# Folding kept partial sums by accumulating transfers instead of VectorE adds, and draining two kept sums earlier

## The chip, the core and the metric

The kernel runs on one core of a Trainium2 chip. The metric is the device time of one execution in microseconds (us); lower is better. The core has a matrix engine (TensorE, "PE" in the profile, with its weight loads "PEld"), a vector engine (VectorE, "DVE"), a scalar engine (ScalarE, "ACT"), a general engine (GpSimd, "POOL") and a sync engine ("SP") which here only issues transfers. All of them run their own instruction list in order and meet at semaphores. Matrix products are written to PSUM, eight banks of 128 x 512 floats; everything else lies in SBUF or in the chip's main memory.

## What is computed

Two decoder layers over 256 tokens of width 2048, in float32. Layer 0 has a short gated convolution, layer 1 latent attention; both end in the same kind of MLP with a squared ReLU, and each sub-layer in a layer norm:

```python
def sq_relu_mlp(x, w1, w2):
    return jnp.square(jax.nn.relu(x @ w1)) @ w2
...
        h = layer_norm(ALPHA * h + mix, ln_g[layer, 0], ln_b[layer, 0])
        h = layer_norm(ALPHA * h + sq_relu_mlp(h, mlp_w1[layer], mlp_w2[layer]),
                       ln_g[layer, 1], ln_b[layer, 1])
```

`w1` is 2048 x 8192 and `w2` is 8192 x 2048. The change touches the MLP of both layers only.

## The kernel before

**Precision.** Every weight that comes in as float32 (`raw`) is split into a rounded part (`hi`, a cast on ACT, L139) and the rest (`lo`, a subtraction on DVE, L140). A product is made of three matmuls: hi by hi, lo by hi, hi by lo. So each 512 KB of weights costs ACT one cast and DVE one 128 x 1024 subtraction.

**The MLP.** The 8192 hidden columns are walked in eight quarters of 1024, numbered q = 0 to 7, each in eight units m = 0 to 7 of 128 columns. A slot (q, m) makes one unit of the first product (`ps_u`, L256 and L260), which ACT and DVE take out of PSUM into `fp` (L401, L402), and, five units behind, one pair of the second product. For the quarters 1 to 6 (`FAST`, in layer 1 also for half of quarter 7) the second product is done by a seven-product scheme in the manner of Strassen: the weights of a pair are combined on DVE (L172, L177, L179), and seven products named "1" to "7" each gather in their own PSUM bank. The output columns are in two groups, g = 0 and g = 1.

**Changes of groups.** At slot (q, 0), q = 2 to 7, the seven banks pass from one group to the other. What they hold is put back into SBUF and what the other group had is brought in. Products "1", "5", "7" and "6" are kept in the tile `sums`, the others in `acc`. ACT copies five of them out (L659) and in (L747). "6" and "4" (`ADDED`) start from zero after a change, and DVE adds them to what is kept: `sums += ps` and `acc += ps`, both at L657. The function `move` takes one entry of the list `moves` at a time, at fixed places of a slot: four at the end of the slot that closes a group, the rest after each single weight of the next slot and behind `evacuate`. Since the list goes by the order 3, 1, 5, 7, 2, 6, 4, the two adds of DVE come last.

**Folds.** When quarter 6 has closed a group, the kept sums are combined by eight dependent adds of 128 x 512 (`fold`, L667): s6 += s1, s7 += s6, then six adds onto blocks of `acc`. `fold` is a generator and `fold_some(n)` runs n of its steps. In layer 0, the eight adds of group 0 run at slot (7, 4) and those of group 1 at (7, 6) and (7, 7). In layer 1 only group 0 is folded so, three adds at (7, 7), two in the slot behind it, and the rest at the end; group 1 is folded with the last products (`fold_last`, L678).

**What hangs on the folds.** In layer 0 the tile `sums` lies in the space of the residual (`xres`). The residual was stored to main memory (`parked`, L895) and comes back as `xback` (L914) by four transfers that POOL issues; they can start only when no fold reads `sums` any more. DVE scales the first part of `xback` (L454), and a matmul on it (`mu0p`, L456) stands in PE's list between the products of the last quarter (`ps_d`). In layer 1 ACT copies the folded blocks of `acc` into PSUM (`last_sum`, `ps_e<-acc`, L685), and the products of the last quarter gather on top.

**Order.** Within the slots the list of each of PE, DVE and ACT is fixed as written (`Order.keep`); POOL and SP, and everything behind the slots, are placed by a scheduler when the program is built. All weights come through seven buffers of 512 KB, loaded by SP.

Of the kernel before, what the change touches and what calls it, by code (L numbers as in the profile page):

```python
# [13 lines left out]
ALU = mybir.AluOpType  # L14
# [8 lines left out]
NQ = 8  # L23
QC = FF // NQ // P
# [13 lines left out]
SHIFT = 5  # L38
# [18 lines left out]
def trunk(ctx: ExitStack, tc: tile.TileContext, xT, vecs, lead, w_first, w_in, w_out, w_kv, w_q, w_uk, w_uv,  # L57
          w_qn, w_qp, w_o, w1, w2, w2f, cosT, sinT, mask, ident, gb, out):
    nc = tc.nc
# [53 lines left out]
    class Banks:  # L113
# [15 lines left out]
        @classmethod  # L129
        def next(cls):  # L130
            cls.count += 1
            return (cls.count - 1) % (4 if cls.more is None else 8)
# [59 lines left out]
    def size(i):  # L192

        return 1 if len(stream[i]) == 1 else 6
# [187 lines left out]
    OWN = ("1", "5", "7", "6")  # L382
# [8 lines left out]
    def fast_products(ps, x, j, fresh, ready, onto=()):  # L391

        b, = take(1, 0)
        a = {n: [x[j // 2][:, j % 2, o, i * P:(i + 1) * P] for o in range(2)] for i, n in enumerate(LEFT, 1)}
        for p, l, r in FACTORS:
            dot(ps[p], b[r], a[l], p in fresh, p in ready, onto=p in onto)
# [197 lines left out]
    for m in range(NC):  # L594
        part = []
        for what in "cub":
            ps = next(pss)
# [23 lines left out]
    def mlp(idx, ln, blocks, fast, begin=None, extra=None, last=False):  # L621
# [14 lines left out]
        def block(n, t):  # L636
            return acc[:, t, n * BW:(n + 1) * BW]
# [11 lines left out]
        def place(p, g):  # L649

            return sums[:, OWN.index(p), g, :] if p in OWN else \
                block(*{"2": (2 * g, 1), "3": (2 * g + 1, 1), "4": (2 * g, 0)}[p])

        def put_back(p, g, ps):

            if p in added:
                nc.vector.tensor_tensor(place(p, g), place(p, g), ps, ALU.add)  # L657
            else:
                nc.scalar.copy(place(p, g), ps)  # L659

        def fold(g):

            s1, s5, s7, s6 = (sums[:, i, g, :] for i in range(4))
            c = [[block(2 * g + b, t) for b in range(2)] for t in range(2)]
            for d, a, b in ((s6, s6, s1), (s7, s7, s6), (c[0][0], c[0][0], s7), (c[0][1], c[0][1], s7),
                            (c[0][1], c[0][1], s5), (c[1][0], c[1][0], s1), (c[1][1], c[1][1], s6), (c[1][1], c[1][1], s5)):
                nc.vector.tensor_tensor(d, a, b, ALU.add)  # L667
                yield

        def fold_last(g):  # L670
# [28 lines left out]
        def forms(u):  # L699

            if q in FAST or last:
                form(u)

        def finish_pair(j, u, at):
            f = factors[j // 2][:, j % 2]
            split(f[:, 0, at], f[:, 1, at], u[:, at])

        q = 0
        for m in range(QC):
            if m < GROUP:  # L710
# [5 lines left out]
                ps = ws[m][1]  # L716
            else:
                ws = [(take(), psum("ps_w"))]
                mm_wide(ws, ln.xd)
                ps = ws[0][1]  # L720
# [12 lines left out]
        ps, onto, fresh, added = {}, set(), set(), set()  # L733
        folds = iter(())

        def resume(p, g, keep=False):

            ps[p] = psum(f"ps_{p}", bank[p])
            onto.discard(p)
            added.discard(p)  # L740
            if p in OWN and opened[g] == FAST[0]:
                fresh.add(p)
            elif p in ADDED and not keep:
                fresh.add(p)
                added.add(p)
            else:
                nc.scalar.copy(ps[p], place(p, g))  # L747
                onto.add(p)
# [3 lines left out]

        moves = []

        def move(n):

            for _ in range(n):
                if moves:
                    o, g, on = moves.pop(0)
                    put_back(o, g, ps[o])  # L760
                    if on:
                        resume(o, 1 - g, last and on == FAST[-1])

        def products_of(p, i, j, g):

            nonlocal folds
            order = [f[0] for f in FACTORS]
            end = j == NB - 1 and (i == 0 or p == FAST[-1] and not last)
            fast_products(ps, factors, j, set(fresh), order if end else (), onto)
            fresh.clear()  # L770
            if end:
                opened[g] = 0
                moves.extend((o, g, p if i == 0 and p < NQ - 1 else 0) for o in order if p < NQ - 1 or o in OWN)
                if p == FAST[-1]:
                    folds = chain(folds, fold(g))

        slots, i = [], state["next"]
        for q, m, pair in steps(last):
            n = (2 if q < NQ else 0) + (pair is not None)
            slots.append((q, m, pair, list(range(i, i + n))))  # L780
            i += n
        order, due = Order(), []

        def split_due():

            while due:
                j, at = due.pop()
                finish_pair(j, rows[j], at)
# [9 lines left out]
        def fold_some(n):  # L798

            for _ in range(n):  # L800
                next(folds, None)

        for s, (q, m, pair, own) in enumerate(slots):
# [6 lines left out]
            singles = [i for i in range(state["next"], end) if i not in own and size(i) == 1 and i not in begun]  # L810
# [32 lines left out]
            ends = q == NQ - 1 and m == QC - 1  # L843
# [2 lines left out]
            to_step(1)  # L846
            if not singles or m == 0 or q == NQ:
                split_due()
            for n, i in enumerate(singles):
                if q == NQ and n == 4:  # L850
                    fold_some(2)
                step(i)
                move(1)
                split_due()
            if crowded:
                evacuate()
                move(len(moves))
            if far:
                for i in far:
                    for _ in range(2):  # L860
                        step(i)
            if q == NQ - 1:
                fold_some((3 if ends else 0) if last else 5 if m == QC - 2 else 3 if ends else 0)
            hi_first = pairs and not crowded and q < NQ
            to_step(1 if hi_first else 2)
            if pair:
                products_of(*pair)
# [14 lines left out]
            if q < NQ:  # L882
                if m % 2 and m < QC - 1 or m == QC - 2:
                    u = rows[m // 2]
                    at = u[:, :T] if m == QC - 2 else u[:, :2 * T]
                    for function in (AF.Relu, AF.Square):
                        nc.scalar.activation(at, at, function)  # L887
                    if m % 2:
                        forms(u)
                    due.extend((m // 2, at) for at in columns(m))  # L890
                if extra and q == FAST[0] and m < NB:
                    for t in range(2):
                        extra(block, m, t, spare[1 + (2 * m + t) % 3])
                if begin and q == FAST[0] and m < 4 and m % 2 == 0:
                    nc.gpsimd.dma_start(parked[:, 4 * m:4 * m + 8, :], held_x[0][:, 4 * m:4 * m + 8, :])  # L895
                if q == NQ - 1 and m == SHIFT - 1 and not last:
                    fold_some(8)
                for i in far:
                    for _ in range(2):
                        step(i)  # L900
            order.keep()
        split_due()
        move(len(moves))
        for _ in folds:
            pass
        h = [factors[j // 2][:, j % 2, :, i * T:(i + 1) * T] for j in range(QC // 2) for i in range(2)]
        if last:
            for n, t, o in ((1, 0, "1"), (0, 1, "5"), (1, 1, "7")):
# [40 lines left out]
    with tc.tile_pool(name="att", bufs=1) as ap:  # L949
# [68 lines left out]
        for m in range(NK):  # L1018
            ps = next(pss)
# [322 lines left out]
```

## Time and profile before

| | |
|---|---|
| median of 3 runs | 2008.2 us (2006.67 to 2009.54) |
| the profiled execution's own time | 2011.46 us |
| its span, first to last instruction | 2009.6 us |
| PE busy | 1990.4 us, 99% |
| DVE busy | 1764.9 us, 88% |
| ACT busy | 1275.1 us, 63% |
| POOL busy | 5.6 us |
| granted TensorE clock, mean | 0.996 |
| transfers | 390 MB, 194 GB/s |

The profiled execution is 1.9 us longer than its span and 3.3 us above the median of the runs. A row of the timeline reads: start, duration, engine, line, operation, result <- operands, shape, count, and in brackets how long the engine sat idle before it and whom it waited for. Matmuls overlap, so what PE loses is seen best in the distance between two starts: 0.23 us for 512 columns.

### The profile page before, as it was taken

The page shows a single profiled execution, that of the slowest core. Times are in us where ns is not written, and L with a number is a line of the kernel's source. Part 1 is how long each engine was busy: PE and PEld are TensorE (multiplying, and loading weights), DVE is VectorE, ACT ScalarE, POOL GpSimd, SP SyncE. Part 2 cuts the span into 40 slices and gives each one's busy share as a digit, 9 for nine tenths or more (in the row PEclk, how much of TensorE's full clock was granted, in tenths as well). Part 3 has the DMA queues.
Part 4 walks back from the last instruction along what each step waited for, and adds up shares of the span by engine and source line. Part 5 has one row for each costly group of instructions (what it writes and reads, how often), then busy time and mean ns, then how long its engine had stood idle before and what let it go on. Part 6 is the DMA issues. An engine that isn't in the chain of part 4 may idle for free.

```text
span 2009.6 us, 29519 instructions
## 1 busy us (share of the span) xinstructions
PE 1990.4 (99%) x11050; PEld 1730.7 (86%) x11050; DVE 1764.9 (88%) x2562; ACT 1275.1 (63%) x1872; POOL 5.6 (0%) x27
## 2 busy tenths in 40 slices
PE   9999999999999999999999999999999999999997
PEld 8888888988888888888879998898888888888885
DVE  8667677777999999999989988777899999999998
ACT  7444445576767767677646655557676776776763
POOL 0000000000000000000000000000000000000000
PEclk9999999999999999999999999999999999999999
DMA  9666666573666566665665544665466656566554
GB/s 343 213 189 190 188 187 191 180 239 127 210 202 197 192 206 209 202 200 193 226 215 178 180 136 136 182 196 170 129 208 208 209 191 208 193 205 210 179 196 149
DMA packets 107711, 389.99 MB, mean 194 GB/s; under 512 B 11952, under 2 KB 12720, under 8 KB 107056
## 3 DMA queue, kind: packets, MB, share of 16 engines
q1 hardware_dynamic: 106560, 383.79, 58.7%
q0 software_dynamic: 864, 4.19, 0.6%
q8 instruction: 86, 1.41, 0.3%
q14 instruction: 57, 0.47, 0.1%
q10 hardware_dynamic: 144, 0.13, 0.0%
HBM read 383.87 MB, written 4.19 MB: 193 GB/s over the span
## 4 chain that ended last, share of the span: by engine, by line
PE 82%; DVE 10%; ACT 5%; issue 3%; DMA 1%; DVEq 0%; ACTq 0%
PE ps_u L256 16%; PE ps_l L256 13%; PE ps_u L260 8%; PE ps_l L260 7%; PE ps L343 6%; PE ps L344 6%; PE ps L341 5%; DVE lo L140 4%; PE ps_d L344 2%; PE ps_d L343 2%; PE ps_d L341 2%; ACT hi L139 2%; PE ps_w L290 1%; PE ps_w L288 1%; PE ps_w L289 1%
## 5 line engine op out<-in xcount | busy, mean ns | idle before, releaser
L140 DVE TENSOR_TENSOR lo<-raw,hi 128x1024 fp32r<-128x1024 f32 x710 | 851.2, 1219 | 122.4 <-ACT hi L139 53.6
L139 ACT CAST hi<-raw 128x1024 fp32r<-128x1024 f32 x710 | 727.4, 1049 | 351.7 <-DVE raw L177 144.5
L256 PE MATMUL ps_u<-xhl,hi 128*128 128x512 f32 x1792 | 622.2, 394 | 4.1 <-DVE fp L402 4.1
L260 PE MATMUL ps_u<-xhl,lo 128*128 128x256 f32 x1792 | 485.6, 280 | 0.0
L256 PEld LDWEIGHTS ps_u<-xhl,hi 128*128 128x128 f32 x1792 | 329.1, 187 | 73.9 <-DVE fp L402 7.4
L260 PEld LDWEIGHTS ps_u<-xhl,lo 128*128 128x128 f32 x1792 | 338.1, 189 | 12.6
L256 PE MATMUL ps_l<-xhl_a,hi 128*128 128x512 f32 x704 | 244.1, 393 | 0.0
L260 PE MATMUL ps_l<-xhl_a,lo 128*128 128x256 f32 x704 | 195.4, 279 | 0.0
L256 PEld LDWEIGHTS ps_l<-xhl_a,hi 128*128 128x128 f32 x704 | 132.1, 188 | 29.9
L260 PEld LDWEIGHTS ps_l<-xhl_a,lo 128*128 128x128 f32 x704 | 131.9, 188 | 0.2
L140 DVE TENSOR_TENSOR lo_t<-raw_t,hi_t 128x1024 fp32r<-128x1024 f32 x100 | 121.8, 1218 | 0.0
L172 DVE TENSOR_TENSOR raw_t<-raw,raw 128x1024 f32<-128x1024 f32 x100 | 121.8, 1218 | 0.0
L401 ACT COPY t<-ps_u 128x256 f32<-128x256 f32 x112 | 41.3, 368 | 101.9 <-PE ps_u L260 101.7
L139 ACT CAST hi_t<-raw_t 128x1024 fp32r<-128x1024 f32 x100 | 105.2, 1052 | 0.0
L256 PE MATMUL ps_l<-z,hi 128*128 128x512 f32 x240 | 82.4, 391 | 0.0
L290 PE MATMUL ps_w<-xd,hi 128*128 128x258 f32 x256 | 72.7, 284 | 0.0
L289 PE MATMUL ps_w<-xd,lo 128*128 128x258 f32 x256 | 72.3, 282 | 0.0
L179 DVE TENSOR_TENSOR raw<-raw 128x512 f32<-128x512 f32 x100 | 69.2, 692 | 3.5
L288 PE MATMUL ps_w<-xd,hi 128*128 128x258 f32 x256 | 72.3, 282 | 0.0
L256 PE MATMUL ps_l<-oT,hi 128*128 128x512 f32 x208 | 71.3, 391 | 0.0
L887 ACT ACTIVATE fp<-fp 128x512 f32<-128x512 f32 (+1 forms) x112 | 64.6, 577 | 7.6 <-DVE fp L402 5.8
L402 DVE TENSOR_TENSOR fp<-ps_u,t 128x256 f32<-128x256 f32 x112 | 46.7, 417 | 25.8 <-ACT t L401 25.6
(363 smaller groups left out, 3897.5 us busy)
## 6 DMA issues: line engine op xcount, KB each, us to landing
raw<-in_w_dram SPq DMA_DIRECT2D x312, 512.0 KB, 4.1
raw<-in_w2f_dram SPq DMA_DIRECT2D x200, 512.0 KB, 4.0
raw<-in_w_in_dram SPq DMA_DIRECT2D x88, 512.0 KB, 3.9
raw<-in_w_out_dram SPq DMA_DIRECT2D x32, 512.0 KB, 3.7
raw<-in_w_o_dram SPq DMA_DIRECT2D x32, 512.0 KB, 4.3
raw<-in_w_kv_dram SPq DMA_DIRECT2D x10, 512.0 KB, 4.6
raw<-in_w_q_dram SPq DMA_DIRECT2D x8, 512.0 KB, 4.4
raw<-in_w_uk_dram SPq DMA_DIRECT2D x8, 512.0 KB, 4.4
```

The costliest lines, as they stand in the source:

```text
L139: nc.scalar.copy(hi, src)
L140: return nc.vector.tensor_tensor(lo, src, hi.bitcast(F32), ALU.subtract)
L172: nc.vector.tensor_tensor(t.rearrange(two, a=2), b12.unsqueeze(1).to_broadcast([P, 2, BW]), r1.rearrange(two, a=2), ALU.subtract)
L179: nc.vector.tensor_tensor(t4, b21, b12, ALU.subtract)
L256: nc.tensor.matmul(ps, w[blk // 8][0][:, blk % 8, :], x, start=first, stop=False)
L260: nc.tensor.matmul(ps[:, :T], w[blk // 8][1][:, blk % 8, :], x[:, :T], start=False, stop=last)
L288: nc.tensor.matmul(ps[:, :W], hi, x[k][:, :W], start=k == 0, stop=False)
L289: nc.tensor.matmul(ps[:, :W], lo, x[k][:, :W], start=False, stop=False)
L290: nc.tensor.matmul(ps[:, :W], hi, x[k][:, W:], start=False, stop=k == NC - 1)
L341: nc.tensor.matmul(ps, x[0], w[0], start=first, stop=False, skip_group_check=onto)
L343: nc.tensor.matmul(ps[:, at], x[0], w[1][:, at], start=False, stop=False, skip_group_check=onto)
L344: nc.tensor.matmul(ps, x[1], w[0], start=False, stop=last, skip_group_check=onto)
```

## The change

Two things are changed. First, the eight adds of `fold` for group 0 are no longer VectorE instructions but transfers from SBUF to SBUF which add to their destination (`accum_op`), issued by POOL; group 1 of layer 0 stays on VectorE. All eight of group 0 are issued at slot (7, 2), in both layers; group 1's are placed at (7, 5) and (7, 6) instead of (7, 6) and (7, 7). Second, a new function `drain` runs after each single weight's step: it puts back all entries of `moves` that are VectorE adds ("6" and "4") at once and leaves the entry in the list with a mark, so that `move` later does only the bringing in.

```diff
             for d, a, b in ((s6, s6, s1), (s7, s7, s6), (c[0][0], c[0][0], s7), (c[0][1], c[0][1], s7),
                             (c[0][1], c[0][1], s5), (c[1][0], c[1][0], s1), (c[1][1], c[1][1], s6), (c[1][1], c[1][1], s5)):
-                nc.vector.tensor_tensor(d, a, b, ALU.add)
+                if g == 0:
+                    nc.gpsimd.dma_start(d, b, accum_op=ALU.add)
+                else:
+                    nc.vector.tensor_tensor(d, a, b, ALU.add)
                 yield
...
+        def drain():
+
+            for k, (o, g, on, full) in enumerate(moves):
+                if o in added and full:
+                    put_back(o, g, ps[o])
+                    moves[k] = o, g, on, False
+
         def move(n):
 
             for _ in range(n):
                 if moves:
-                    o, g, on = moves.pop(0)
-                    put_back(o, g, ps[o])
+                    o, g, on, full = moves.pop(0)
+                    if full:
+                        put_back(o, g, ps[o])
                     if on:
                         resume(o, 1 - g, last and on == FAST[-1])
...
-            for n, i in enumerate(singles):
-                if q == NQ and n == 4:
-                    fold_some(2)
+            for i in singles:
                 step(i)
                 move(1)
+                drain()
                 split_due()
             if crowded:
                 evacuate()
                 move(len(moves))
+            if q == NQ - 1 and m == SHIFT and not last:
+                fold_some(4)
+            if q == NQ - 1 and m == 2:
+                fold_some(8)
...
-            if q == NQ - 1:
-                fold_some((3 if ends else 0) if last else 5 if m == QC - 2 else 3 if ends else 0)
+            if q == NQ - 1 and m == QC - 2 and not last:
+                fold_some(4)
...
-                if q == NQ - 1 and m == SHIFT - 1 and not last:
-                    fold_some(8)
...
-        for _ in folds:
-            pass
```

DVE's list at one of the changes of groups, before (`lo` is a weight's rest, `fp` the unit taken out of PSUM, `raw_t` a combination of the next pair):

```order
L172 TENSOR_TENSOR raw_t<-raw_1_7587,raw_0_7585 128x1024
L140 TENSOR_TENSOR lo_7592<-raw_7548,hi_7591 128x1024
L140 TENSOR_TENSOR lo_7599<-raw_7550,hi_7598 128x1024
L657 TENSOR_TENSOR sums_4784<-sums_4784,ps_6815 128x512
L402 TENSOR_TENSOR fp<-ps_u,t 128x256
L657 TENSOR_TENSOR acc_4113<-acc_4113,ps_6820 128x512
L140 TENSOR_TENSOR lo_1_7610<-raw_0_7585,hi_1_7609 128x1024
```

and DVE's list at the same place of the changed kernel:

```order
L172 TENSOR_TENSOR raw_t<-raw_1_7587,raw_0_7585 128x1024
L140 TENSOR_TENSOR lo_7592<-raw_7548,hi_7591 128x1024
L657 TENSOR_TENSOR sums_4784<-sums_4784,ps_6816 128x512
L657 TENSOR_TENSOR acc_4113<-acc_4113,ps_6820 128x512
L140 TENSOR_TENSOR lo_7601<-raw_7550,hi_7600 128x1024
L402 TENSOR_TENSOR fp<-ps_u,t 128x256
L140 TENSOR_TENSOR lo_1_7610<-raw_0_7585,hi_1_7609 128x1024
```

Both adds to kept sums moved ahead of the second `lo`; nothing was added or removed here.

DVE's list in the slots (7, 4) to (7, 7) of layer 0, before (`h1a` is the split of the hidden columns):

```order
L402 TENSOR_TENSOR fp<-ps_u,t 128x256
L667 TENSOR_TENSOR sums_4784<-sums_4784 128x512 x2
L667 TENSOR_TENSOR acc_4113<-acc_4113,sums_4784 128x512 x6
L140 TENSOR_TENSOR lo_9554<-raw_9516,hi_9553 128x1024
L140 TENSOR_TENSOR lo_9559<-raw_9518,hi_9558 128x1024
L657 TENSOR_TENSOR sums_4784<-sums_4784,ps_9179 128x512
L402 TENSOR_TENSOR fp<-ps_u,t 128x256
L657 TENSOR_TENSOR acc_4113<-acc_4113,ps_9184 128x512
L140 TENSOR_TENSOR lo_9607<-raw_9569,hi_9606 128x1024
L140 TENSOR_TENSOR h1a_4515<-fp,h1a_4515 128x512
L140 TENSOR_TENSOR lo_9613<-raw_9571,hi_9612 128x1024
L667 TENSOR_TENSOR sums_4784<-sums_4784 128x512 x2
```

and of the changed kernel:

```order
L402 TENSOR_TENSOR fp<-ps_u,t 128x256
L140 TENSOR_TENSOR lo_9554<-raw_9516,hi_9553 128x1024
L657 TENSOR_TENSOR sums_4784<-sums_4784,ps_9180 128x512
L657 TENSOR_TENSOR acc_4113<-acc_4113,ps_9184 128x512
L140 TENSOR_TENSOR lo_9561<-raw_9518,hi_9560 128x1024
L402 TENSOR_TENSOR fp<-ps_u,t 128x256
L670 TENSOR_TENSOR sums_4784<-sums_4784 128x512 x2
L670 TENSOR_TENSOR acc_4113<-acc_4113,sums_4784 128x512 x2
L140 TENSOR_TENSOR lo_9611<-raw_9573,hi_9610 128x1024
L140 TENSOR_TENSOR h1a_4515<-fp,h1a_4515 128x512
L140 TENSOR_TENSOR lo_9617<-raw_9575,hi_9616 128x1024
L670 TENSOR_TENSOR acc_4113<-acc_4113,sums_4784 128x512 x4
```

The eight adds of group 0 left DVE's list, and those of group 1 end ahead of the unit of (7, 6); before, the last three of them stood two units further on.

POOL's list from the return of the residual on, with both layers, in the changed kernel (the rows of L668 are new, the others stood in this order before):

```order
L909 DMA parked<-xres 128x2048 x2
L668 DMA acc_4113<-sums_4784 128x512
L668 DMA sums_4784<-sums_4784 128x512 x2
L668 DMA acc_4113<-sums_4784 128x512 x5
L924 DMA xback<-parked 128x1024 x4
L968 MEMSET kpe 128x512
L668 DMA acc_13773<-sums_14490 128x512
L668 DMA sums_14490<-sums_14490 128x512 x2
L668 DMA acc_13773<-sums_14490 128x512 x5
```

The four transfers that bring the residual back now stand behind eight accumulating ones in POOL's list.

More of the change, by code (lines that the diff above doesn't have):

```diff
@@ L772, in products_of @@
                 opened[g] = 0
-                moves.extend((o, g, p if i == 0 and p < NQ - 1 else 0) for o in order if p < NQ - 1 or o in OWN)
+                moves.extend((o, g, p if i == 0 and p < NQ - 1 else 0, True) for o in order if p < NQ - 1 or o in OWN)
                 if p == FAST[-1]:
```

## The prediction

> **What bounds the kernel now.** I read the page first, then PE's waits, then the timeline around each of them.
>
> ```profile
> PE 1990.4 (99%) x11050; PEld 1730.7 (86%) x11050; DVE 1764.9 (88%) x2562; ACT 1275.1 (63%) x1872; POOL 5.6 (0%) x27
> ...
> PE ps L1225 <- ACT umeans L1222: 4.8, 1, 4.8
> PE ps_u L256 <- DVE fp L402: 4.1, 7, 2.1
> PE mu0p L456 <- DVE xback L454: 2.8, 1, 2.8
> ...
> PE ps L341 <- ACT ps L747: 0.9, 1, 0.9
> PE ps L341 <- ACT h3a L139: 0.8, 1, 0.8
> PE ps L344 <- DVE h3a L140: 0.6, 1, 0.6
> ```
>
> PE is busy 99% of the span, so a change of DVE's work can win only what PE loses by waiting. These are all waits of PE over 0.5 us but its start. All but the first come from DVE being late at a change of groups or near a fold. So the gain has a ceiling of some 15 us, and each place has to be looked at by itself.
>
> ```profile
> 708.00:792.00 84.00, 83.49 (x426) 70.58 (x424) 82.34 (x101) 58.93 (x78) 0.00 (x0) 1.00 0.62 202
> ```
>
> The table by stretch (columns: window, length, busy PE, PEld, DVE, ACT, POOL, clock, DMA share, GB/s) has DVE busy 82.3 of 84 us between two changes of groups: it keeps pace with PE with hardly 2% to spare, and 1 us lost there reaches PE.
>
> **Part 1: the two adds put forward at a change of groups.** The change at slot (4, 0) in layer 0, PE first, then DVE:
>
> ```profile
> 707.89 0.39 PE L344 MATMUL ps<-t,h1c 128*128 128x512 f32 x1
> 708.63 0.50 PE L256 MATMUL ps_u<-xhl,hi 128*128 128x512 f32 x1 [0.35 <-DVE fp L402]
> ...
> 691.54 1.23 DVE L140 TENSOR_TENSOR lo<-raw,hi 128x1024 fp32r<-128x1024 f32 x1 [0.25 <-ACT hi L139]
> 693.62 1.23 DVE L140 TENSOR_TENSOR lo<-raw,hi 128x1024 fp32r<-128x1024 f32 x1 [0.85 <-ACT hi L139]
> 694.76 0.68 DVE L657 TENSOR_TENSOR sums<-sums,ps 128x512 f32<-128x512 f32 x1
> ...
> 695.69 0.68 DVE L657 TENSOR_TENSOR acc<-acc,ps 128x512 f32<-128x512 f32 x1
> 696.29 1.22 DVE L140 TENSOR_TENSOR lo<-raw,hi 128x1024 fp32r<-128x1024 f32 x1
> ...
> 708.16 0.41 DVE L402 TENSOR_TENSOR fp<-ps_u,t 128x256 f32<-128x256 f32 x1
> ```
>
> PE's starts are 0.74 us apart where 0.23 is the rule, and the product that restarts takes 0.50 instead of 0.39: 0.6 us lost, because `fp` frees the unit's bank at 708.57. DVE has no gap between 693.62 and there, but one of 0.85 us just before, while it waits for the second cast. The two adds (0.6 us from start to start) now stand in that gap: they run from 692.77 to about 693.95, the second `lo` follows at once, and the row that began at 696.29 begins at about 695.35. DVE is 0.9 us earlier, more than the 0.6 us that PE waits. Three such changes in layer 0 and three in layer 1 (q = 4 to 6; at q = 2 and 3 only one add exists and PE doesn't wait) are six of the seven waits of `ps_u` above: 6 x 0.6 = 3.6 us. Bounds: 0, if ACT is what DVE then waits for, and 3.6.
>
> At q = 7 in layer 1 the late adds cost more, since ACT brings both sums back behind them:
>
> ```profile
> 1897.68 0.59 ACT L747 COPY ps<-sums 128x512 f32<-128x512 f32 x1 [1.89 <-DVE sums L657]
> ...
> 1900.30 0.50 PE L341 MATMUL ps<-t,h3c 128*128 128x512 f32 x1 [0.86 <-ACT ps L747]
> ...
> 1901.25 1.23 DVE L140 TENSOR_TENSOR lo<-raw,hi 128x1024 fp32r<-128x1024 f32 x1 [1.63 <-ACT hi L139]
> ...
> 1911.29 0.39 PE L344 MATMUL ps<-t,h3c 128*128 128x512 f32 x1
> 1913.73 0.50 PE L256 MATMUL ps_u<-xhl,hi 128*128 128x512 f32 x1 [2.06 <-DVE fp L402]
> ```
>
> PE loses 1.1 us at 1900 and 2.3 us at 1912. ACT waits 1.89 us for the add, then DVE waits 1.63 us for ACT's next cast, behind it. With the adds ahead ACT goes on 1.9 us sooner and that `lo` begins at about 1898.3, 2.9 us earlier. PE, without the first stall, wants the bank 1.1 us sooner, so some 0.4 us of 3.4 stay: 3.0 us. Bounds 1.1 and 3.4.
>
> **Part 2: group 0's folds leave DVE.**
>
> ```profile
> 979.45 3.95 DVE L667 TENSOR_TENSOR acc<-acc,sums 128x512 f32<-128x512 f32 x6
> ...
> 985.34 0.37 ACT L401 COPY t<-ps_u 128x256 f32<-128x256 f32 x1 [4.64 <-PE ps_u L260]
> ...
> 1002.52 0.69 DVE L667 TENSOR_TENSOR acc<-acc,sums 128x512 f32<-128x512 f32 x1
> ...
> 1003.74 1.64 POOL L914 DMA_DIRECT2D xback<-parked  x3 [564.16 <-DVE fp L402]
> ...
> 1011.26 0.29 DVE L454 TENSOR_SCALAR xback<-xback 128x256 f32<-128x256 f32 x1 [3.65 <-DMA xback<-parked]
> ...
> 1008.24 0.61 PE L344 MATMUL ps_d<-hi,h1a 128*128 128x512 f32 x2
> 1011.61 1.22 PE L456 MATMUL mu0p<-xback,ones 128*128 128x256 f32 x2 [2.76 <-DVE xback L454]
> ...
> 1018.01 0.40 PE L344 MATMUL ps_d<-hi,h1c 128*128 128x512 f32 x1
> ...
> 1011.60:1018.00 6.40, 6.39 (x15) 5.08 (x16) 6.40 (x10) 1.42 (x2) 1.02 (x2) 0.51 1.01 394
> ```
>
> In layer 0 the last fold ends at 1003.2, POOL starts the return of the residual at 1003.74, it lands 7.5 us later, and PE has nothing else in its list. It waits 2.8 us and then runs 6.4 us at a granted clock of 0.51. From 1008.47 (the second of the x2) to 1018.01 pass 9.54 us for 14 products at 0.23 and two small ones of about 0.3: 3.8 us of work. So 5.7 us are lost.
>
> The rule of the Trainium skill (TensorE: Matmul & The Clock Gate, Part 1) is that the clock falls to half after an idle window of about 3.4 us. By it a wait of 2.8 us would not slow the clock and its end would return 2.8 us, not 5.7; the granted clock of 0.51 behind this wait shows that here it does.
>
> Now the eight adds of group 0 (from 978.0 to 983.3) are gone. Group 1's first four wait for `fp` of slot (7, 5), whose unit ends at 985.3: they run from 986.0 to 988.6, two `lo` and a split follow, the other four run to about 994. `xback` can start at 994.5 instead of 1003.7 and, with the same 7.5 us, is there at 1002; DVE scales it behind one more `lo`, near 1005.5, before PE comes to `mu0p` at 1008. I take 5.4 of the 5.7 us; bounds 0 (another wait in its place) and 5.7.
>
> In layer 1 the folds stood in DVE's unbroken run ahead of the last products of the scheme:
>
> ```profile
> 1959.47 1.41 DVE L667 TENSOR_TENSOR sums<-sums 128x512 f32<-128x512 f32 x2
> 1960.80 1.28 DVE L667 TENSOR_TENSOR acc<-acc,sums 128x512 f32<-128x512 f32 x2
> ...
> 1963.47 0.68 DVE L667 TENSOR_TENSOR acc<-acc,sums 128x512 f32<-128x512 f32 x1
> ...
> 1965.58 0.39 PE L344 MATMUL ps<-t,h3a 128*128 128x512 f32 x1
> 1966.79 0.50 PE L341 MATMUL ps<-hi,h3a 128*128 128x512 f32 x1 [0.82 <-ACT h3a L139]
> ...
> 1968.12 0.50 PE L344 MATMUL ps<-hi,h3a 128*128 128x512 f32 x1 [0.60 <-DVE h3a L140]
> ```
>
> Five adds, 3.1 us, stand ahead of the split `h3a` for which PE stalls: from 1965.58 to 1968.12 are 2.54 us for three products of 0.23, near 2.0 us lost with what follows. Without them the split is 2 us earlier: 2.0 us (bounds 1 and 2). Two more adds go from the tail, where DVE works without a pause until the last statistics, just behind PE's last product: 1.2 us less work, of which about 0.6 count before PE itself is the later one (bounds 0 and 0.6). One was hidden in a wait at 1894.9 and is worth nothing. SP's list only swaps the last loads of gains and one weight: nothing, covered by the same queue.
>
> **What the transfers cost.** No row shows an accumulating transfer.
>
> ```profile
> parked<-xres POOLq DMA_DIRECT2D x2, 1024.0 KB, 6.7
> xback<-parked POOLq DMA_DIRECT2D x4, 512.0 KB, 8.5
> ...
> out_dram<-acc SPq DMA_DIRECT2D x8, 256.0 KB, 2.4
> ...
> 1969.05 0.58 ACT L685 COPY ps_e<-acc 128x512 f32<-128x512 f32 x1
> ```
>
> Each moves 256 KB and reads its target too. The lower bound is 2.4 us, a plain one of that size; the upper 17, twice the 8.5 of 512 KB in a busy time. I take 6, near POOL's own 6.7. The chain s6, s7, then two adds onto one block, is four in a row, 24 us. In layer 0 it begins at about 945 and must end by 994: four of up to 12 us are free, and `xback` would start at its old time at 14.7. In layer 1 it begins near 1895, and ACT's first copy of `acc` into PSUM, at 1969 now and 5 us earlier with the gains ahead of it, wants it near 1964: up to 17 us each. POOL does nothing else then, so its waits hold up only `xback`. The transfers share the engines with the weights, which keep them 62% busy; the sixteen add about 8 MB read and 4 MB written. I take 1.5 us for late weights (bounds 0 and 8, 1 us in each of the eight slots they cover).
>
> By the Trainium skill (DMA: Bandwidth & Descriptors, Anatomy of one DMA) a transfer of POOL takes 2.0 us plus its bytes over 436 GB/s; as an estimate 2.6 us here, which would leave the sum as it is.
>
> Sum: 3.6 + 3.0 + 5.4 + 2.0 + 0.6 - 1.5 = 13.1 us. The profiled execution, 2011.46 us with 1.9 around its span, would take 1998.4; the runs' median lies 3.3 below it, so I forecast 2008.2 - 13.1 = 1995.1 us.
>
> **Rivals.**
>
> *Weights come late.* A transfer of POOL takes turns with the weight loads on the same sixteen engines. Each slot's pair is combined on DVE some 2 us after it lands, and DVE has no slack in layer 1's quarter 7. At 1 us in each of eight slots the sum is 14.6 - 8 = 6.6: 2001.6 us. For it: DVE's 82.3 of 84. Against: loads wait for buffers, not for the engines.
> The Trainium skill says so of the engines (DMA: Bandwidth & Descriptors, Issuing engines are not separate DMA queues); no run here has measured the price.
>
> *Nothing comes of it.* DVE is off the path but for short stalls; if ACT's casts hold DVE at the changes and `mu0p` finds a new wait, the time stays: 2008 us. Against: each stall above names DVE.
>
> *Slow accumulation (slower).* If one accumulating transfer takes 20 us, the chain ends at 945 + 80 = 1025; `xback` is there 22 us later than now and DVE, in order, stands before it with the next weights' `lo` behind. Layer 1's copy waits to 1975, 11 us late. 33 us, less the 8 us won elsewhere: +25, 2033 us. It decides from about 15 us per transfer in layer 0. For it: the add is done on the way, and no row shows its rate. Against: a megabyte took POOL 6.7 us.
>
> **How the numbers follow.** The forecast has 0.62, late weights 0.18, nothing 0.08, slow accumulation 0.12 (a mild one, at 16 to 18 us, still costs over 4 us net only with some late weights, and I count it here). A change under 0.2% (4 us) can't be told from none. The range holds the first two cases: from 1991.5, all bounds of the gain, to 2004. Faster 0.79, same 0.09, slower 0.12.
>
> **What would show it.** PE's waits for `fp` of L402 and for `xback` L454 gone, no stretch at half clock near 1012, `xback` issued near 995; POOL's transfers landing in 3 to 10 us; layer 1's stalls at 1900, 1912 and 1966 gone. It would be wrong if `xback` still starts after 1000, or if DVE's `raw_t` begins to wait for transfers.

## The result, and the profile after

| | before | after |
|---|---|---|
| median (lowest to highest) | 2007.4 us (2006.2 to 2009.5), 4 runs | 1996.8 us (1996.1 to 1996.9), 4 runs |
| ratio | 1 | 0.9945, 95% interval 0.9928 to 0.9962 |
| the same pair, compared again | 2008.5 us (2007.8 to 2012.0), 9 runs | 1996.1 us (1994.6 to 1998.2), 5 runs |
| ratio there | 1 | 0.9934, 95% interval 0.9921 to 0.9946 |
| span of the profiled execution | 2009.6 us | 1995.1 us |

By the medians the change wins 10.7 us in the first comparison and 12.5 in the second (by the ratios 11.0 and 13.3); the forecast was 1995.1 us, 13.1 less than the median it started from. One run of the version with another end took 2170.5 us at a granted clock of 0.85 and is left out of its numbers below. The two profiled executions lie 14.5 us apart in their spans, because the profiled one of before was slower than its own median. All sums below are of profiled executions unless they say median.

The page of the changed kernel, its first part, and then PE's waits of over 0.2 us, but the start's:

```profile
PE 1984.8 (99%) x11050; PEld 1730.0 (87%) x11050; DVE 1755.7 (88%) x2546; ACT 1278.5 (64%) x1872; POOL 19.7 (1%) x43
```

```profile
PE ps L1235 <- ACT umeans L1232: 4.1, 1, 4.1
...
PE ps_e L341 <- ACT hi L139: 0.5, 1, 0.5
PE ps_u L256 <- DVE fp L402: 0.3, 1, 0.3
```

Of the waits that the prediction listed, the one at the end is left, and a small one of `ps_u`. The wait for `mu0p`, the wait for ACT's copies of kept sums at the last change and those for `h3a` are gone. One is new: `ps_e` waits for a cast, 0.5 us. DVE's busy time fell by only 9.2 us of 1764.9; the span fell by 14.5, since what counted was where DVE was late, not how much it had to do.

The timeline of POOL, and the place where `xback` comes back, in the changed kernel:

```profile
941.45 0.91 POOL L668 DMA_DIRECT2D acc<-sums  x1 [501.45 <-ACT acc L659]
947.91 0.88 POOL L668 DMA_DIRECT2D sums<-sums  x1 [5.54 <-DVE raw L179]
...
979.04 0.87 POOL L668 DMA_DIRECT2D acc<-sums  x1 [8.19 <-issue]
986.24 0.87 POOL L668 DMA_DIRECT2D acc<-sums  x1 [6.33 <-issue]
993.21 1.65 POOL L924 DMA_DIRECT2D xback<-parked  x3 [6.10 <-DVE fp L402]
...
1003.08 0.29 DVE L454 TENSOR_SCALAR xback<-xback 128x256 f32<-128x256 f32 x1
...
1005.53 0.59 PE L456 MATMUL mu0p<-xback,ones 128*128 128x256 f32 x2
```

And the stretch behind it in the table by stretch:

```profile
1005.50:1012.00 6.50, 6.50 (x30) 5.35 (x29) 6.45 (x14) 2.95 (x5) 0.00 (x0) 1.00 1.02 412
```

`xback` is issued at 993.2 (the forecast said 994.5), DVE scales it at 1003.1 without waiting, and PE comes to `mu0p` at 1005.5 without waiting; the granted clock there is 1.00 where it was 0.51. But the eight transfers are not four in a row beside four others: each starts 4 to 9 us after the one before it, the last at 986.2. By the landing times each starts 0.3 to 0.4 us after the one before it has landed: the one issued at 970.0 lands 8.7 us later, at 978.7, and the next starts at 979.0.

They also show in the transfers' list (KB each, median us from issue to landing):

```profile
acc<-sums POOLq DMA_DIRECT2D x12, 256.0 KB, 5.5
...
xback<-parked POOLq DMA_DIRECT2D x4, 512.0 KB, 6.6
sums<-sums POOLq DMA_DIRECT2D x4, 256.0 KB, 6.0
```

### The profile page after: what moved, and what is told of

Read it like the earlier page. It is cut to its first block, busy times and chain, and to the rows that moved or that the text cites. A ratio compares the mean times of both kernels' runs of the same rounds, so it can differ in the third digit from the quotient of the medians.

```text
span 1995.1 us, 29544 instructions
## 1 busy us (share of the span) xinstructions
PE 1984.8 (99%) x11050; PEld 1730.0 (87%) x11050; DVE 1755.7 (88%) x2546; ACT 1278.5 (64%) x1872; POOL 19.7 (1%) x43
## 3 DMA queue, kind: packets, MB, share of 16 engines
q0 software_dynamic: 3168, 8.39, 1.7%
## 4 chain that ended last, share of the span: by engine, by line
PE 94%; DVE 3%; ACT 1%; DMA 1%; issue 1%; DVEq 0%; ACTq 0%
PE ps_u L256 20%; PE ps_l L256 13%; PE ps_u L260 10%; PE ps L343 7%; PE ps L344 7%; PE ps L341 7%; PE ps_l L260 7%; PE ps_d L344 2%; PE ps_d L343 2%; PE ps_d L341 2%; PE ps_w L290 1%; PE ps_w L288 1%; PE ps_w L289 1%; DVE lo L140 1%; PE ps_g L288 1%; PE ps_g L290 1%
## 5 line engine op out<-in xcount | busy, mean ns | idle before, releaser
L402 DVE TENSOR_TENSOR fp<-ps_u,t 128x256 f32<-128x256 f32 x112 | 46.9, 418 | 27.7 <-ACT t L401 27.5
L140 DVE TENSOR_TENSOR t<-raw,t 128x512 fp32r<-128x512 f32 x100 | 68.5, 685 | 2.1 <-ACT t L139 1.6
```

The costliest lines, as they stand in the source:

```text
L140: return nc.vector.tensor_tensor(lo, src, hi.bitcast(F32), ALU.subtract)
```

## Experiments

The theory: the change removes separate stalls, and what the prediction listed adds up. The rivals: the adds alone or the transfers alone do it; putting folds early counts, not the engine that does them; the transfers cost late weights. Ratios are against runs of the kernel before on the same chip, where it had medians of 2008.5 to 2010.0 us. The runs were made on several chips, so a difference of medians between two of them can also hold a difference of chips; where that matters, the ratios stand beside it.

### Each part alone

The kernel before with `drain` and the marks in `moves` alone:

```diff
                 step(i)
                 move(1)
+                drain()
                 split_due()
```

> The kernel before, with only part 1 of the change: the two adds put forward at each change of groups; all folds stay on VectorE at their old places. My theory (the terms of the prediction are separate and add up): the six group changes and the last one of layer 1 are won, 3.6 + 3.0 = 6.6 us, so 2007.4 - 6.6 = 2000.8 us (1999.5 to 2002.5), PE's waits of L256 for fp shrink from 4.1 us in 7 to under 1 us, and the 2.8 us wait for xback with its stretch at half clock stays as it was. Rival 1 (putting the adds forward is all there is to the change, the transfers only cover their own cost): as fast as the changed kernel, 1996.8 us. Rival 2 (the adds are not what PE waits for; the transfers did it all): 2007 us.

Measured: 2003.3 us (2000.7 to 2004.0), ratio 0.9961 (0.9949 to 0.9974); the medians lie 6.7 us apart. PE's waits, but the start's:

```profile
PE ps L1234 <- ACT umeans L1231: 4.6, 1, 4.6
PE mu0p L456 <- DVE xback L454: 3.2, 1, 3.2
...
PE ps L341 <- ACT h3a L139: 0.8, 1, 0.8
PE ps L344 <- DVE h3a L140: 0.6, 1, 0.6
```

All seven waits of `ps_u` are gone from the list, and the ones for `xback` and `h3a` stand as before: 6.6 us were expected of this part, and 6.7 came by the medians, 7.8 by the ratio.

The changed kernel without `drain()`:

```diff
                 move(1)
-                drain()
                 split_due()
```

> The changed kernel without part 1: transfers and the new places of the other folds stay, the adds to kept sums stand where they stood before. My theory: the group changes stall again (PE's waits of L256 for fp back at about 4 us in 7, and the 3.4 us at the last change of layer 1), so 1996.8 + 6.6 = 2003.4 us (2001.5 to 2004.5), with no wait for xback and no stretch at half clock. Rival 1 (the adds are all): 2007 us. Rival 2 (the transfers did it all): 1997 us.

Measured: 2003.9 us (2002.0 to 2004.5), ratio 0.9964 (0.9952 to 0.9977). PE's waits:

```profile
PE ps_u L256 <- DVE fp L402: 4.1, 7, 2.1
PE ps L1234 <- ACT umeans L1231: 4.1, 1, 4.1
...
PE ps L341 <- ACT ps L750: 0.9, 1, 0.9
PE ps_e L341 <- ACT hi L139: 0.8, 1, 0.8
```

The seven waits are back to a tenth, and neither `xback` nor `h3a` is among them. In these lists the parts don't overlap: each leaves the other's waits about as they were. By the ratios they win 0.39% and 0.36%, and both together, in the comparison that follows, 0.66% with an interval of 0.54 to 0.79, which holds their sum. (The first comparison, with fewer runs, gave 0.55%, 0.38 to 0.72, which doesn't quite.)

The changed kernel once more, beside nine runs of before:

> The changed kernel, unchanged, on the chip of the runs that follow, to read its gain against more runs of the kernel before. The first comparison gave 0.9945 (11.0 us) against four runs of before; parts 1 and 2 alone gave 7.8 and 7.2 us on another chip, with medians of before of 2010.0. If the terms add up, the gain here is 13 to 15 us, a ratio of 0.9930 (0.9920 to 0.9940), and the small gain of the first comparison came of the few runs of before. Rival: the parts overlap (a stall that either of them removes), and the gain is 10 to 11 us again, 0.9948.

Measured: ratio 0.9934 (0.9921 to 0.9946), 12.5 us by the medians. By the ratio that is within the theory's range and by the medians between theory and rival; with the two waits lists above it speaks for the sum.

### The same places, on VectorE

```diff
-                if g == 0:
+                if g > 1:
                     nc.gpsimd.dma_start(d, b, accum_op=ALU.add)
```

> The changed kernel with every fold on VectorE: order and places as in the changed kernel, no transfer, so the eight adds of group 0 stand in one run in slot (7, 2) of each layer. My theory: VectorE is busy 9.9 of 10 us there (the stretches 885 to 915), so eight adds of 0.61 us from start to start, 4.9 us, reach PE nearly whole, about 4.5 us in each layer; the late weights of layer 1 (1 us) go. 1996.8 + 9 - 1 = 2005 us (2002 to 2008). Rival 1 (putting the folds early is what counts, not the engine): 1997 us. Rival 2 (the transfers cost by late weights about what the adds cost): 1996 to 1998 us.

Measured: 2008.2 us (2006.4 to 2009.2), ratio 0.9989 (0.9980 to 0.9998), so all that the change wins is lost again but 0.1%. PE's waits have it at the two places where the eight adds stand:

```profile
PE ps_u L256 <- DVE fp L402: 8.8, 2, 5.4
```

The first, in layer 0, is 3.3 us, the second 5.4; 9 us were expected.

The wait for `xback` is not in this kernel's list either: `xback` is issued at 996.8 and PE comes to `mu0p` 12.4 us later, where before it had 5.0 us, and the 3.6 us that PE lost in between are not all of the difference. So in layer 0 it is the earlier places of the folds that take this wait away, and the transfers that keep the eight adds from costing PE at the new place. That leaves a rival untried: group 0's adds left on VectorE at (7, 4), where in the kernel before PE lost only 0.2 us behind them (at 985), and group 1's alone put earlier.

Transfers in layer 0 alone:

```diff
-                if g == 0:
+                if g == 0 and not last:
                     nc.gpsimd.dma_start(d, b, accum_op=ALU.add)
```

> The changed kernel with transfers in layer 0 alone; in layer 1 the eight adds of group 0 go to VectorE in one run in slot (7, 2). My theory: layer 0 as in the changed kernel; in layer 1 PE stalls some 4.5 us near 1890 and the weights are not late (1 us back): 1996.8 + 3.5 = 2000.3 us (1998.5 to 2002). Rival (late weights: in layer 1 the transfers cost as much as they save): 1996 to 1998 us, with VectorE's waits for w2f and ACT's for raw back near zero.

Measured: 2004.0 us (2002.1 to 2004.3), ratio 0.9964 (0.9952 to 0.9977). By the medians that is 7 to 8 us over the changed kernel, by the ratios 4 to 6; 3.5 were expected. Its profile is 7.4 us longer than the first one of the changed kernel. The timeline of DVE and PE in this kernel, in order of time, and the stretch behind it:

```profile
1899.53 1.42 DVE L670 TENSOR_TENSOR sums<-sums 128x512 f32<-128x512 f32 x2
1900.65 0.39 PE L344 MATMUL ps<-t,h3c 128*128 128x512 f32 x1
1900.98 3.95 DVE L670 TENSOR_TENSOR acc<-acc,sums 128x512 f32<-128x512 f32 x6
1904.85 1.22 DVE L140 TENSOR_TENSOR lo<-raw,hi 128x1024 fp32r<-128x1024 f32 x1
...
1906.45 0.80 PE L256 MATMUL ps_u<-xhl,hi 128*128 128x512 f32 x1 [5.41 <-DVE fp L402]
```

```profile
1906.40:1911.30 4.90, 4.85 (x15) 4.17 (x16) 4.87 (x6) 4.27 (x5) 0.00 (x0) 0.50 0.14 18
```

The eight adds take 5.3 us, and PE loses 5.6 of them (5.80 from start to start, less 0.23): nothing is hidden. What the expectation left out is the clock: PE runs the next 4.9 us at 0.50, which costs it some 2.4 us more. So the place is good only for an engine that has time there, and in layer 1 the transfers are worth 4 to 8 us against VectorE at the same place; in layer 0 they are worth 4.3 us (2004.0 beside the 2008.2 above, on the same chip). Against the old places on VectorE (the first run, ratio 0.9961, beside 0.9945 and 0.9934) they are worth 3 to 5 us in both layers together by the ratios, some 7 by the medians.

### What a transfer costs

Plain transfers in place of accumulating ones (they overwrite their target, so the adding itself is left out):

```diff
-                    nc.gpsimd.dma_start(d, b, accum_op=ALU.add)
+                    nc.gpsimd.dma_start(d, b)
```

> The changed kernel with plain transfers of the same size and places in place of the accumulating ones (the folds of group 0 are left out: the sums are overwritten, not added). Theory (an accumulating transfer is dear because its target is read too): landing falls from 5.5 to 6.0 us to 3 to 4, the chain in layer 0 ends before 975 instead of 993, the stalls at 1921 and 1965 in layer 1 shrink and the time is 0.5 to 1.5 us less, 1995.5 us. Rival (the price is that of POOL's issue and of the queue's start and end): landing within 0.5 us of the accumulating one and the same time, 1996.8 us.

Measured: 1996.1 us (1995.6 to 1996.4), ratio 0.9933 (0.9918 to 0.9949). The transfers' list and POOL's timeline in this kernel:

```profile
acc<-sums POOLq DMA_DIRECT2D x12, 256.0 KB, 4.8
...
sums<-sums POOLq DMA_DIRECT2D x4, 256.0 KB, 4.2
```

```profile
948.37 0.55 POOL L668 DMA_DIRECT2D sums<-sums  x1 [5.22 <-DMA sums<-sums]
948.92 0.55 POOL L668 DMA_DIRECT2D acc<-sums  x1
952.02 1.11 POOL L668 DMA_DIRECT2D acc<-sums  x2 [2.56 <-DMA sums<-sums]
...
992.96 1.62 POOL L924 DMA_DIRECT2D xback<-parked  x3 [33.75 <-DVE fp L402]
```

A plain transfer lands 0.7 to 1.8 us sooner, so adding makes a single transfer only that much longer. What differs is that plain ones are issued one behind the other, 0.55 us apart, when nothing that they need is under way. The last of them is issued at 958.7, not 986, and the time is the same: in the changed kernel the chain is just hidden, and `xback` waits for DVE's own folds here (`fp` at L402 stands behind them).

Group 1's folds of layer 0 by transfers too:

```diff
-                if g == 0:
+                if g == 0 or not last:
                     nc.gpsimd.dma_start(d, b, accum_op=ALU.add)
```

> The changed kernel with group 1's eight folds of layer 0 by transfers too: sixteen in one queue, each behind the one before, and the return of the residual behind the last. My theory (the slow chain of the prediction's third rival, with the length of the chain doubled instead of the price): eight took from 941 to 993, 6.5 us each; the second eight begin near 993 and end near 1040, xback lands 7 us later, near 1047, and PE, which stands before mu0p from 1006, waits some 40 us, while VectorE wins 5 us: 1996.8 + 38 = 2035 us (2020 to 2045), PE's wait for xback L454 of 30 us or more. Rival 1 (transfers overlap but for those that depend on each other): chain of five, some 25 us from 984, xback at 1016, 2006 us. Rival 2 (the transfers are hidden whatever their number): 1992 to 1997 us.

Measured: 2026.6 us (2024.3 to 2028.4), ratio 1.0085 (1.0071 to 1.0098): slower by 17 us than before by the ratio, 18 by the medians. POOL's timeline and PE:

```profile
1008.05 0.86 POOL L668 DMA_DIRECT2D acc<-sums  x1 [4.03 <-DMA sums<-sums]
1011.56 0.88 POOL L668 DMA_DIRECT2D acc<-sums  x1 [2.65 <-issue]
1015.10 0.86 POOL L668 DMA_DIRECT2D acc<-sums  x1 [2.66 <-issue]
...
1026.41 1.65 POOL L924 DMA_DIRECT2D xback<-parked  x3 [3.33 <-DMA acc<-sums]
...
1031.13 1.22 PE L456 MATMUL mu0p<-xback,ones 128*128 128x256 f32 x2 [25.75 <-DVE xback L454]
```

The sixteen come one after the other and PE waits 25.7 us, as the theory said; it was 8 us too dear, since the transfers come faster while PE stands still and no weights are loaded: 3.5 us apart from 1008 on. They keep that distance where the profile shows no wait for any transfer ("issue").

Eight more accumulating transfers in layer 1, between dead sums:

```diff
                 yield
+            if last and g == 0:
+                for _ in range(8):
+                    nc.gpsimd.dma_start(s1, s5, accum_op=ALU.add)
+                    yield
...
             if q == NQ - 1 and m == 2:
-                fold_some(8)
+                fold_some(16 if last else 8)
```

> The changed kernel with eight more accumulating transfers of 256 KB in layer 1, from a dead sum onto another dead one, in POOL's queue among and behind the eight real ones; the order on the other engines is the same. It prices what such transfers cost the weights. Theory (the wait of ACT for a weight near 1965 comes of weight loads that start when buffers come free, not of the transfers, since it stands with plain transfers too, that had ended by 1903): eight more cost 0 to 1 us, 1996.4 to 1997.4 us, and the stalls of PE near 1921 and 1965 stay 0 to 1 us. Rival (the prediction's late weights, 1 us in each slot that the transfers cover): eight slots more are covered, +5 to +8 us, 2002 to 2004 us, with waits of ACT for raw and of VectorE for w2f in each.

Measured: 1997.8 us (1996.3 to 1999.2), ratio 0.9943 (0.9930 to 0.9957). ACT and PE in this kernel:

```profile
1965.96 1.04 ACT L139 CAST hi<-raw 128x1024 fp32r<-128x1024 f32 x1 [2.51 <-DMA raw<-in_w_dram]
...
1963.95 0.40 PE L341 MATMUL ps_e<-hi,h3c 128*128 128x512 f32 x1
1967.05 0.50 PE L341 MATMUL ps_e<-hi,h3c 128*128 128x512 f32 x1 [2.71 <-ACT hi L139]
```

The eight cost 1.0 to 1.7 us by the medians; by the ratios (beside 0.9945 and 0.9934) nothing to 1.8, so the size is not clear of the noise. In the profile what they cost is at one place: near 1965 the wait grows from 0.5 to 2.7 us, and 3.2 us at a clock of 0.51 follow. From 1885 to 1960, beside the transfers, PE shows no stall but 0.36 us at 1900. So transfers do make a weight late where one is wanted early, but not slot by slot.

### The new wait near 1965

The four last loads of gains in POOL's queue:

```diff
-            nc.sync.dma_start(gbt[:, n, :], gb[n].partition_broadcast(P))
+            nc.gpsimd.dma_start(gbt[:, n, :], gb[n].partition_broadcast(P))
```

> The changed kernel with the four last loads of gains (512 KB each) in POOL's queue and not in SP's, where two of them stand between the last weights at 1955.0; the order of the last products on PE and of VectorE's splits changes a little with it. Theory (the new stall near 1965 comes of SP's order: three weights go out at 1956.0 behind two loads of gains, and ACT waits 0.9 to 1.3 us for the first): the wait of ACT for raw near 1965 and PE's stall of 0.5 to 0.8 us go, 1996.4 - 0.7 = 1995.7 us (1995 to 1996.4). Rival (the weights wait for buffers that VectorE frees late, whatever stands in the queue): the stall stays, 1996.4 us.

Measured: 1997.9 us (1996.1 to 1999.6), ratio 0.9942 (0.9929 to 0.9954). The theory falls. ACT now waits sooner and longer (its timeline), and PE waits for the copies that stand behind this cast in ACT's list (PE's waits):

```profile
1960.53 1.05 ACT L139 CAST hi<-raw 128x1024 fp32r<-128x1024 f32 x1 [2.51 <-DMA raw<-in_w_dram]
```

```profile
PE ps_e L341 <- ACT ps_e L688: 1.4, 1, 1.4
```

The order of the last products changed with this edit too, so it doesn't tell whether it was the queue, the two megabytes of gains or the buffers. It stays open why that weight is late; with plain transfers, all issued by 1900, PE still loses 0.56 us there, so it is not the accumulating. Whether it is the transfers at all is open too: the two kernels above without transfers in layer 1 but with the folds at the new place don't show this wait, but there PE had lost some 8 us near 1900 and wanted the weight that much later.

### A version that beats both

The long wait that is left, 4.1 us for `umeans`, stands behind four scalings of the other half's output in DVE's list. They were written behind the second half's last products:

```diff
                 for i in order:
                     centred(i)
-                    scaled(i, us[i], gbt[:, i, BW:])
+                later.extend((i, lambda i=i: scaled(i, us[i], gbt[:, i, BW:])) for i in order)
                 return
...
             store(t, one)
+            for _, f in later:
+                f()
```

> The changed kernel with another order at its end: the four scalings of the first half's output (2.7 us of VectorE, at 1981.4 in the changed kernel) are written behind the second half's last products, so that the order puts the second half's mean and variance behind one of them and not behind four. Theory: the 4.1 us for which PE waits for umeans become about 2, and the products behind it start 2 us earlier; if the clock then stays full, their starts are 0.23 apart and not 0.86, which wins up to 3 us more. 1996.4 - 2 = 1994.4 us with the half clock, 1991.5 without (1991 to 1995). Rival (the end is set by VectorE's work and the stores, whatever their order): 1996 to 1997 us.

Measured: 1993.0 us (1992.6 to 1993.2), ratio 0.9919 (0.9904 to 0.9934). The end in the changed kernel, then in this one:

```profile
1984.84 3.78 PE L1235 MATMUL ps<-gbt,umeans 128*128 128x512 f32 x4 [4.10 <-ACT umeans L1232]
```

```profile
1982.28 1.98 PE L1235 MATMUL ps<-gbt,umeans 128*128 128x512 f32 x4 [2.11 <-ACT umeans L1232]
```

The wait falls by 2 us, and the first four products behind it take half the time: the granted clock is 1.00 from 1979 to 1990 here, where it was 0.52 from 1984 to 1990. The version is about 3 us faster than the changed kernel (0.9919 beside 0.9934).

With the gains in POOL's queue added to it:

> The kernel with the reordered end (1993.1 us) with the same move of the four loads of gains to POOL's queue. Theory (the two savings are at different places and add up): PE's stall near 1964, 1.07 + 0.11 us there, goes, 1992.2 us (1991.5 to 1993.0). Rival: 1993.1 us, no change.

Measured: 1995.3 us (1993.1 to 1997.7), ratio 0.9929 (0.9915 to 0.9943), no gain; PE waited 2.3 us for ACT's copies near 1965.

### The kernel before, a second profile

> The kernel before, profiled a second time. Theory (its runs differ by what the clock does behind PE's wait for xback, which the prediction costed at 5.7 us from one execution): the wait is again 2.5 to 3.5 us, but the stretch at a clock of 0.5 behind it has another length than 6.4 us, between none and 6.4, and with it the loss is between 2.6 and 5.7 us. Rival (always the same stretch; the runs differ elsewhere): 6.4 us at 0.51 again, 5.7 us lost.

Measured: 2010.1 us. PE's timeline at `mu0p` and at the last change of layer 1, the stretches behind the two waits, and what PE's list of waits has left of `h3a`:

```profile
1011.82 0.70 PE L456 MATMUL mu0p<-xback,ones 128*128 128x256 f32 x2 [2.84 <-DVE xback L454]
...
1912.61 0.50 PE L256 MATMUL ps_u<-xhl,hi 128*128 128x512 f32 x1 [2.11 <-DVE fp L402]
```

```profile
1013.00:1016.30 3.30, 3.30 (x9) 2.54 (x9) 3.30 (x7) 0.79 (x1) 0.00 (x0) 0.50 1.02 411
...
1913.80:1917.00 3.20, 3.20 (x12) 2.77 (x11) 3.20 (x5) 3.20 (x5) 0.00 (x0) 0.55 0.10 36
```

```profile
PE ps L344 <- DVE h3a L140: 0.2, 1, 0.2
```

The wait for `xback` is the same to 0.1 us, but only 3.3 us follow at half clock instead of 6.4, so the place cost 4.7 us and not 5.7. And the wait of 2.1 us at 1912, behind which the first profile had a full clock, is followed here by 3.2 us at 0.55, another 1.6 us lost. That loss is made up for later: of the two waits for `h3a`, 1.4 us in the first profile, 0.2 us are left here. The last change and `h3a` together cost 5.4 us in the first profile and 5.5 in this one.

## Why the prediction was right

**Part 1, six changes of groups, 3.6 us.** Right. They cost 0.61 us each with the adds late (in both profiles of before and without `drain`), none with it: 3.7.

**Part 1, the last change of layer 1, 3.0 us.** Right: 1.1 and 2.3 us lost before, 0.4 left, 3.1 won. What stays is the 0.4 that the prediction left. (In the second profile of before the half clock behind the wait made the loss 1.6 us larger.)

**Part 2, layer 0, 5.4 us.** Right for the execution that it was read from: the products from 1008.47 to 1018.01 took 9.55 us there and take 3.66 in the changed kernel, so 5.9 us went. For a median it is too much by up to 1 us: the second profile lost 4.7 and the run with `drain` alone 4.9 (3.4 for the wait, 1.5 behind it). That can be part of the gap between 13.1 and the measured 10.7 to 12.5; two further profiles don't show how much of it. The sum was made from one execution and taken off the median of others.

**Part 2, layer 1 ahead of `h3a`, 2.0 us, and SP's list, nothing.** The 2.0 us went, but 0.6 to 0.8 came back at the same place as a wait for a late weight, which was not in the sum: with `h3a` on time the cast of that weight was late next. The term also varies: in the second profile of before only 0.5 us were lost at `h3a`, because PE, held up 1.6 us longer at the last change, came to it later (VectorE and ACT were no sooner with it). So this stall and the one at the last change are not independent, as the sum took them to be. The prediction dismissed SP's list as covered; the wait is of a weight from that list, though the run that moved the gains didn't bear out their order as its cause.

**The tail, 0.6 us.** Right: PE's loss there (from one start to the next, less 0.23) was 4.95 us and became 4.26 in the profile; it was 4.78 in the second one of before.

**Late weights, -1.5 us.** Roughly right as a sum, wrong as a mechanism. One of the prediction's signs of being wrong came, in a small form: VectorE's `raw_t` waits for weights beside the transfers, 1.6 us in two waits in the first profile of the changed kernel (before 1906 and 1926, in layer 1) and 2.1 us in the second (before 952, in layer 0), and not in the kernel before or with all folds on VectorE. PE has one short stall behind them in each profile, 0.6 us at 1921 in the first and 0.5 us at 957 in the second. Eight more transfers cost at most some 2 us, all at 1965. "1 us in each of eight slots" happened nowhere.

Terms with their measured sizes in the two first profiles: 3.7 + 3.1 + 5.9 + 2.0 + 0.7 = 15.4, less 0.8 and 0.6 for the two new stalls, 14.0 of the 14.5 us between the two spans. The lower end of the range, 1991.5 us, was not what the bounds add up to: 3.6 + 3.4 + 5.7 + 2.0 + 0.6 = 15.3, or 1992.9 us.

**The transfers' price and the room for them.** The price was right (6 us taken, 5.5 and 6.0 measured), the room was wrong. The prediction counted the dependent ones, four in a row, and gave each 12 us in layer 0, with slow accumulation deciding from 15. In fact all eight come one at a time, and in the second profile of the changed kernel it is the last of them, issued at 988.9, that releases `xback`:

```profile
996.06 1.65 POOL L924 DMA_DIRECT2D xback<-parked  x3 [6.29 <-DMA acc<-sums]
...
1003.17 0.28 DVE L454 TENSOR_SCALAR xback<-xback 128x256 f32<-128x256 f32 x1
...
1005.63 0.59 PE L456 MATMUL mu0p<-xback,ones 128*128 128x256 f32 x2
```

DVE scales at 1003.2 what PE wants at 1005.6: 2 to 3 us of room in all, 0.3 us for each of eight. The rival of slow accumulation decides from some 7 us between transfers and not from 15, and it came about when there were sixteen. That the forecast held is luck in this part: with the wrong count of transfers in a row, it held by a margin of some 0.3 us for each.

## What to carry to other kernels

Where an engine has no slack, a few late instructions at one place cost more than many elsewhere: find the stall, then ask which instruction ahead of it can be done sooner or by somebody else; the same adds at the new place on VectorE cost all the gain. Count transfers of one queue one after another unless a trace shows that they overlap, and compare the end of the whole row with when its last reader comes. Two stalls of the same stretch are not always separate: where PE was held 1.6 us longer at the first, the second was shorter by 1.5. A stall's price is the wait and the slow clock behind it; the second part varies from run to run, so read it from more than one profile before it goes into a sum.

## What the chip showed that was not expected

**Accumulating transfers do not overlap on POOL's queue.** Their starts were never less than 3.5 us apart (256 KB each, weights standing still), 3.7 to 9 beside weight loads, also where the profile shows no wait for one of them. In all nine profiles with such transfers each one starts 0.31 to 0.40 us after the one before it has landed. Plain ones of the same size followed at 0.55 us. The issue takes 0.87 us and not 0.55, and POOL's queue (q0, software_dynamic in the page) moves 144 packets for each and not 80 ((3168 - 864) / 16 and (2144 - 864) / 16, 864 being the count before). What makes the next one wait for the landing was not tried.

**The same wait is followed by very different stretches at half clock.** In the kernel with the folds on VectorE, PE's timeline at the stall in layer 0, and the stretch behind it:

```profile
960.75 0.50 PE L256 MATMUL ps_u<-xhl,hi 128*128 128x512 f32 x1 [3.34 <-DVE fp L402]
```

```profile
960.70:964.00 3.30, 3.25 (x18) 2.86 (x19) 3.27 (x5) 2.67 (x4) 0.00 (x0) 1.00 0.00 0
```

A wait of 3.3 us with the clock at 1.00 behind it; 2.8 us with 6.4 and with 3.3 us at half; 2.1 us with none and with 3.2. The Trainium skill (TensorE: Matmul & The Clock Gate, Part 1) says that the activity window runs freely and isn't started by the kernel, and the spread agrees with that; its figure of an idle window of about 3.4 us does not cover the wait of 2.1 us here.
